# A two-layer decoder trunk on one core: sums of weights formed in place, a fourth landing buffer, one PSUM bank per step in the cross output projection, six pairs by seven products

## The chip, the core and the metric

The kernel runs on one core of a Trainium2 chip. A core has TensorE (matrix products, PE in the profile; PEld is its weight load), VectorE (DVE), ScalarE (ACT), GpSimd (POOL) and SyncE (SP, whose queue issues all DMAs here). The metric is the device time of one execution in microseconds, and less is better. Beside the times there is one profiled execution, whose rows this document quotes.

## What is computed

Two layers over 256 tokens of width 2048, all in float32:

```python
for l in range(2):
    h = rms_norm(x, attn_norm[l])
    q, k, v, ... = split(h @ w_in[l])                 # 6 MoBA, 4 differential, 6 DSA heads, an indexer
    x = x + concat(moba, diff, dsa) @ w_out[l]
    h, m = rms_norm(x, cross_norm[l]), rms_norm(mem, mem_norm[l])
    x = x + cross_attention(h @ cross_wq[l], m @ cross_wkv[l]) @ cross_wo[l]    # 4 heads, width 512
    u = rms_norm(x, ffn_norm[l]) @ ffn_w_up[l]        # 2048 -> 2 * 5504
    g, val = split(causal_conv3(u, ffn_conv_w[l]) + ffn_conv_b[l])
    x = x + (silu(g) * val) @ ffn_w_down[l]           # 5504 -> 2048
```

## The kernel before, in words

**Splitting.** Each operand of a large product is split into a rounded part and the rest: `hi` is made by ACT (line 79), `lo = raw - hi` by DVE (line 81). A product is then three matmuls: hi by hi, hi by lo, lo by hi. So every weight goes through one chain: SP issues the DMA into a `raw` buffer, ACT writes `hi`, DVE writes `lo`, PE reads both. There are three `raw`, three `hi` and three `lo` buffers of 8 KB per partition (`RAWS`, `HIS`), used in turn; a buffer is reused when its last reader is done. Activations are split in the same way (`parts`, lines 266 and 267, into tiles `a`).

**Order of the work.** The Tile framework keeps every engine's instructions in one fixed order, chosen when the program is built from priorities (the order of the code) and from when it expects data to be ready. Within an engine nothing overtakes: an instruction that waits holds back all behind it. Small chains (attention, norms) are written as generators; `step` runs one to its next `yield n`, and `tick` lets it go on after `n` groups of matmuls, so they lie between the matmuls of the next large product.

**Down projection** (`down`). `ffn_w_down` has 43 row blocks of 128: 21 pairs and one single. The output is made in two groups `g` of 1024 columns in each layer, so there are four groups in all. A group goes through the pairs in order, with the single one put in between. A *plain* pair takes 4 outputs x 2 row blocks x 3 = 24 matmuls of 512 columns. A pair whose number is in `SEVEN` goes by seven products of sums instead of eight (Winograd's form of Strassen's scheme): 7 x 3 = 21 matmuls, but DVE also forms four sums of weight blocks (lines 303 to 305, into a tile `sum` of its own, one buffer), sums of activations (298 to 301, tile `t`), and must split two sets of weights: the blocks themselves (`w`, 3 x 512) and the sums (`wt`, 4 x 512). Such a pair is called a seven below. A group ends with `combine` (lines 327 to 345: DVE adds the eight banks), and layer 0 then turns the result into the transposed residual `xT` (lines 1075 to 1080), while layer 1 writes it out by DMA (line 1064, on the SP queue like the loads).

**Output projections** (`residual`, `up_acc`). The transposed residual `xT` is updated in 8 steps of two column blocks. A step takes two PSUM banks out of four of the tag `mm`. In the cross output projection (`whole=True`) a step has 4 row blocks x 2 x 3 = 24 matmuls of 256 columns, and fills only half of each of its two banks; DVE adds each half bank to `xT` (line 437), then `take` splits the new `xT` for the next product (ACT line 180, DVE line 186) and sums its squares (ACT, then POOL line 408). After the 8 steps `factors` waits `G_R` ticks, multiplies the sums of squares by ones on PE (line 416) and forms the reciprocal root on DVE; after the cross output projection `spread` then brings it to all partitions (PE line 1007).

**Constants.** The convolution weights have one tile per layer (`cw0`, `cw1`), and the gains of the heads for both layers lie in three tiles (`gbd`, `gbs`, `gbm`) from the start on; `rope_table` multiplies them with sines and cosines on POOL. There are 8 tiles of the tag `t`, and 38 of the tag `k` (`slot`).

Of the kernel before, what the change touches and what calls it, by code (L numbers as in the profile page):

```python
# [10 lines left out]
F32 = mybir.dt.float32  # L11
# [9 lines left out]
L = 2  # L21
# [7 lines left out]
NEG = -1.0e30  # L29
GONE = -3.0e38  # L30
TOPK = 64
G_R, G_T, G_S, G_PT, G_DN = 3, 5, 1, 3, 3
FIRST_COL = 3328
KP, AP, RAWS, HIS = 38, 8, 3, 3
SEVEN = frozenset((2, 5, 8, 11, 14, 16, 18))
GW = 2 * CH


# [5 lines left out]
def hybrid_trunk(ctx: ExitStack, tc: tile.TileContext, x, mem, positions, attn_norm, w_in,  # L44
# [28 lines left out]
    def new_raw(a, n):  # L73
        return wp.tile([P, a, n], F32, tag="raw", name="raw", bufs=RAWS)

    def halves(src, a, n):

        hi = wp.tile([P, a, n], F32R, tag="hi", name="hi", bufs=HIS)
        nc.scalar.activation(hi, src, AF.Copy)  # L79
        lo = wp.tile([P, a, n], F32R, tag="lo", name="lo", bufs=HIS)  # L80
        nc.vector.tensor_tensor(lo, src, hi.bitcast(F32), OP.subtract)  # L81
        return hi, lo


# [41 lines left out]
    def attn_g(l):  # L126
        return gA[:, l * KT:(l + 1) * KT]

    def load_conv(l):
        cw = cst.tile([P, 4, 2 * NF], F32, name=f"cw{l}")  # L130
# [12 lines left out]
        return cw  # L143

# [83 lines left out]
    def up_acc(wview, runs, acts, order=None, whole=False):  # L228


        outs = [pmm() for _ in range(2)]
        order = order or EIGHTS
        first = True
        for gi, grp in enumerate(order):
            n = len(grp)
            hi, lo = load_split([wview[:, grp[0]:grp[0] + n, c:c + m] for c, m in runs], n, 2 * P)
            for j, k in enumerate(grp):
                last = gi == len(order) - 1 and j == n - 1
                for i in range(2):
                    wh, wl = hi[:, j, i * P:(i + 1) * P], lo[:, j, i * P:(i + 1) * P]  # L240
                    if whole:
                        nc.tensor.matmul(outs[i][:, :S], lhsT=wh, rhs=acts[k][:, :S], start=first, stop=False)
                        nc.tensor.matmul(outs[i][:, :S], lhsT=wh, rhs=acts[k][:, S:], start=False, stop=False)
                    else:
                        nc.tensor.matmul(outs[i], lhsT=wh, rhs=acts[k], start=first, stop=False)  # L245
                    ins = nc.tensor.matmul(outs[i][:, :S], lhsT=wl, rhs=acts[k][:, :S], start=False,  # L246
                                           stop=last)
# [22 lines left out]
    def down(act, wview, col, order):  # L270
# [16 lines left out]
        for i in order:  # L287
            m = width(i)
            k = 2 * i
            if i in SEVEN:  # L290
# [8 lines left out]
                                        OP.subtract)  # L299
                nc.vector.tensor_tensor(s4[:, 2, :], s4[:, 1, :], a4[:, 0, :], OP.add)  # L300
                nc.vector.tensor_tensor(s4[:, 3, :], a4[:, 2, :], s4[:, 2, :], OP.subtract)
                tt = wp.tile([P, 4, CH], F32, tag="sum", name="sum", bufs=1)
                nc.vector.tensor_tensor(tt[:, 0:2, :], b[:, 1::2, :], b[:, 0:1, :].to_broadcast([P, 2, CH]), OP.add)  # L303
                nc.vector.tensor_tensor(tt[:, 2, :], tt[:, 1, :], b[:, 1, :], OP.add)
# [7 lines left out]
                todo = {1: (A(0), B(0)), 2: (A(2), B(1)), 3: (Sx(3), B(2)), 4: (A(3), T(3)), 5: (Sx(1), T(0)),  # L312
                        6: (Sx(2), T(2)), 7: (Sx(0), T(1))}
                for q in (1, 2, 3, 5, 7, 6, 4):
                    ins = product(q, *todo[q])
            else:
# [92 lines left out]

    def factors(acc, rest=None):  # L410

        yield G_R
        pt = pat()
        for t in range(NT):
            for j in range(2):
                nc.tensor.matmul(pt[:, t:t + 1], lhsT=acc[:, j * S + t * P:j * S + (t + 1) * P],
                                 rhs=ones[:, 0:1], start=(j == 0), stop=(j == 1))
# [10 lines left out]
    def residual(acts, wview, order, g, tiles, rest=None, whole=False):  # L428

        acc = new_acc()  # L430
        for i in range(KT // 2):
            outs = up_acc(wview, [(2 * i * P, 2 * P)], acts, order[i], whole)
            pair = xT[:, 2 * i:2 * i + 2, :].rearrange("p k s -> p (k s)")
            if whole:
                for j in range(2):
                    v = xT[:, 2 * i + j, :]
                    nc.vector.tensor_tensor(v, outs[j][:, :S], v, OP.add)  # L437
# [70 lines left out]
        nc.gpsimd.tensor_copy(ropeI[:, 1, :, 0, 32:], s)  # L508

    TAB_W = {"d": 64, "s": 128, "m": 128}  # L510
    head_gain = {}
    for kind, g in (("d", diff_qk_gain), ("s", dsa_qk_gain), ("m", moba_qk_gain)):
        gb = cst.tile([P, L, 2, TAB_W[kind]], F32, name="gb" + kind)
        nc.sync.dma_start(gb.rearrange("p l a d -> p (l a d)"),
                          g.rearrange("l a d -> (l a d)").unsqueeze(0).to_broadcast([P, L * 2 * TAB_W[kind]]))
        head_gain[kind] = gb
# [15 lines left out]
    def rope_table(l, kind):  # L532

        w = TAB_W[kind]
        st, h = 128 // w, w // 2
        gb = head_gain[kind][:, l]
# [235 lines left out]
    for l in range(L):  # L772
# [239 lines left out]
        cw = load_conv(l)  # L1012


        up = ffn_w_up[l].rearrange("(k p) n -> p k n", p=P)
# [96 lines left out]
```

## Time and profile before

| | |
|---|---|
| median of 3 runs | 2567.83 us (2561.11 to 2570.95) |
| the profiled execution's own time | 2556.22 us |
| its span (first to last instruction) | 2554.4 us |
| PE busy | 98% |
| DVE busy | 75% |
| ACT busy | 53% |
| mean share of 16 DMA engines | 55.8% |
| mean granted TensorE clock | 0.997 |
| down projection, layer 0 and layer 1 | about 1039 to 1279 us, and 2307 to 2551 us |

The times are in us from the start of the span. In a list of groups a row has the line, the engine, the operation, the tiles (written<-read), the shapes and the count; behind the bar are the busy time, the mean in ns, and the idle time of the engine just before these instructions with what ended it. In a timeline a row has start, duration, engine, line and operation, and in square brackets how long the engine had been idle and what it waited for. In the chain of waits a row has the total, the count and the longest. A window row has the busy time of PE, its number of matmuls, the granted clock, the share of the DMA engines and GB/s. A matmul's duration is longer than its distance to the next, since matmuls are pipelined.

### The profile page before, as it was taken

The page shows a single profiled execution, that of the slowest core. Times are in us where ns is not written, and L with a number is a line of the kernel's source. Part 1 is how long each engine was busy: PE and PEld are TensorE (multiplying, and loading weights), DVE is VectorE, ACT ScalarE, POOL GpSimd, SP SyncE. Part 2 cuts the span into 40 slices and gives each one's busy share as a digit, 9 for nine tenths or more (in the row PEclk, how much of TensorE's full clock was granted, in tenths as well). Part 3 has the DMA queues.
Part 4 walks back from the last instruction along what each step waited for, and adds up shares of the span by engine and source line. Part 5 has one row for each costly group of instructions (what it writes and reads, how often), then busy time and mean ns, then how long its engine had stood idle before and what let it go on. Part 6 is the DMA issues. An engine that isn't in the chain of part 4 may idle for free. (4 is left out here: it accounts for less than half of the span.)

```text
span 2554.4 us, 34687 instructions
## 1 busy us (share of the span) xinstructions
PE 2514.4 (98%) x13402; PEld 2146.4 (84%) x13402; DVE 1910.2 (75%) x2982; ACT 1364.4 (53%) x1756; POOL 162.8 (6%) x177
## 2 busy tenths in 40 slices
PE   8999999999999999999999999999999999999999
PEld 7778888888888888877787788888888888888777
DVE  6876766677777777889968767666777777778888
ACT  5555565455554555556545555554555555555554
POOL 2210101010000000000041011010100000000000
PEclk9999999999999999999999999999999999999999
DMA  7545546555566656555654555564556665664554
GB/s 240 165 151 177 167 153 201 166 168 189 183 197 186 193 188 192 173 198 173 215 162 146 164 170 164 161 213 133 185 186 193 188 192 184 196 189 163 192 195 152
DMA packets 377705, 459.89 MB, mean 180 GB/s; under 512 B 10638, under 2 KB 331076, under 8 KB 377540
## 3 DMA queue, kind: packets, MB, share of 16 engines
q1 hardware_dynamic: 377540, 457.67, 55.8%
q8 instruction: 105, 1.72, 0.3%
q14 instruction: 60, 0.49, 0.1%
HBM read 455.54 MB, written 2.10 MB: 179 GB/s over the span
## 5 line engine op out<-in xcount | busy, mean ns | idle before, releaser
L81 DVE TENSOR_TENSOR lo<-raw,hi 128x2048 fp32r<-128x2048 f32 (+4 forms) x466 | 969.7, 2084 | 356.0 <-ACT hi L79 354.7
L245 PE MATMUL mm<-k,hi 128*128 128x512 f32 x3136 | 1098.4, 393 | 3.2 <-DVE xT L437 3.2
L79 ACT ACTIVATE hi<-raw 128x2048 fp32r<-128x2048 f32 (+4 forms) x466 | 811.2, 1744 | 434.5 <-PE mm L221 164.0
L246 PE MATMUL mm<-k,lo 128*128 128x256 f32 x3264 | 914.4, 280 | 0.1
L245 PEld LDWEIGHTS mm<-k,hi 128*128 128x128 f32 x3136 | 586.8, 187 | 133.2 <-issue 3.5
L246 PEld LDWEIGHTS mm<-k,lo 128*128 128x128 f32 x3264 | 617.1, 189 | 0.8 <-DVE lo L81 0.5
L220 PE MATMUL mm<-hi,k 128*128 128x512 f32 (+2 forms) x1088 | 413.8, 380 | 0.0
L221 PE MATMUL mm<-hi,k 128*128 128x512 f32 (+2 forms) x1088 | 404.3, 372 | 0.0
L222 PE MATMUL mm<-lo,k 128*128 128x512 f32 (+2 forms) x1088 | 401.6, 370 | 1.0 <-DVE lo L81 1.0
L220 PEld LDWEIGHTS mm<-hi,k 128*128 128x128 f32 x1088 | 206.3, 190 | 35.8 <-issue 3.3
L222 PEld LDWEIGHTS mm<-lo,k 128*128 128x128 f32 x1088 | 205.5, 189 | 36.1 <-DVE lo L81 1.8
L221 PEld LDWEIGHTS mm<-hi,k 128*128 128x128 f32 x1088 | 206.3, 190 | 32.6 <-issue 2.6
L285 PE MATMUL mm<-lo,a 128*128 128x512 f32 x548 | 216.4, 395 | 15.7 <-DVE lo L81 15.7
L283 PE MATMUL mm<-hi,a 128*128 128x512 f32 x548 | 214.6, 392 | 0.2 <-DVE t L1027 0.2
L284 PE MATMUL mm<-hi,a 128*128 128x512 f32 x548 | 214.4, 391 | 0.0
L1040 ACT ACTIVATE t<-t 128x256 f32<-128x256 f32 x86 | 35.7, 418 | 229.3 <-DVE t L1032 229.3
L285 PEld LDWEIGHTS mm<-lo,a 128*128 128x128 f32 x548 | 103.5, 189 | 43.2 <-DVE lo L81 21.9
L1027 DVE TENSOR_TENSOR t<-mm,t 128x256 f32<-128x256 f32 x172 | 68.8, 421 | 90.3 <-ACT t L1024 90.3
L1024 ACT ACTIVATE t<-mm 128x256 f32<-128x256 f32 x172 | 60.2, 375 | 142.2 <-PE mm L246 142.2
L408 POOL TENSOR_TENSOR k<-k,t 128x512 f32<-128x512 f32 x35 | 52.2, 1492 | 1138.0 <-ACT t L407 976.1
L283 PEld LDWEIGHTS mm<-hi,a 128*128 128x128 f32 x548 | 103.7, 189 | 21.6 <-issue 0.6
L284 PEld LDWEIGHTS mm<-hi,a 128*128 128x128 f32 x548 | 103.6, 189 | 21.8
(242 smaller groups left out, 2571.7 us busy)
## 6 DMA issues: line engine op xcount, KB each, us to landing
raw<-in_ffn_w_up_dram SPq DMA_DIRECT2D x168, 1024.0 KB, 5.1
raw<-in_w_in_dram SPq DMA_DIRECT2D x152, 512.0 KB, 4.5
raw<-in_ffn_w_down_dram SPq DMA_DIRECT2D x56, 1024.0 KB, 5.6
raw<-in_w_in_dram SPq DMA_DIRECT2D x20, 1024.0 KB, 5.0
raw<-in_w_out_dram SPq DMA_DIRECT2D x16, 1024.0 KB, 5.5
raw<-in_cross_wkv_dram SPq DMA_DIRECT2D x16, 1024.0 KB, 5.0
raw<-in_ffn_w_down_dram SPq DMA_DIRECT2D x32, 512.0 KB, 5.2
raw<-in_ffn_w_down_dram SPq DMA_DIRECT2D x56, 256.0 KB, 3.8
```

Of the source, the lines that this page charges most:

```text
L79: nc.scalar.activation(hi, src, AF.Copy)
L81: nc.vector.tensor_tensor(lo, src, hi.bitcast(F32), OP.subtract)
L220: nc.tensor.matmul(o, lhsT=xh, rhs=hi[:, j, :], start=first, stop=False)
L221: nc.tensor.matmul(o, lhsT=xl, rhs=hi[:, j, :], start=False, stop=False)
L222: ins = nc.tensor.matmul(o, lhsT=xh, rhs=lo[:, j, :], start=False, stop=last)
L245: nc.tensor.matmul(outs[i], lhsT=wh, rhs=acts[k], start=first, stop=False)
L246: ins = nc.tensor.matmul(outs[i][:, :S], lhsT=wl, rhs=acts[k][:, :S], start=False, stop=last)
L283: nc.tensor.matmul(bank[q], lhsT=x[0], rhs=w[0], start=first, stop=False)
L284: nc.tensor.matmul(bank[q], lhsT=x[1], rhs=w[0], start=False, stop=False)
L285: return nc.tensor.matmul(bank[q], lhsT=x[0], rhs=w[1], start=False, stop=left[q] == 0)
L1024: nc.scalar.activation(uv[:, S:], outs[i][:, S:], AF.Copy)
L1027: nc.vector.tensor_tensor(u, outs[i][:, :S], v, OP.add)
```

## The change

Seven edits, which belong together through the memory that they free and use:

1. The sums of weights are formed in place, in the `raw` buffer of the pair, after `w` is split; the tile `sum` goes. They are four additions of 512, and `wt` is split in two halves, each with one ACT and one DVE instruction.
2. `raw` and `hi` have four buffers, `lo` still three; `t` has seven instead of eight.
3. `SEVEN` is 2, 5, 8, 11, 14, 17 instead of 2, 5, 8, 11, 14, 16, 18: six pairs, three apart.
4. In the cross output projection a step uses one bank, its two halves beside each other, and DVE adds the whole bank to `xT` in one instruction.
5. `factors` waits five ticks instead of three, but three as before after the cross output projection.
6. There is one tile for the convolution weights, loaded anew in layer 1.
7. The heads' gains are loaded for each layer into `k` tiles; in layer 1 this puts three small DMAs between the loads of the indexer's second half.

```diff
-G_R, G_T, G_S, G_PT, G_DN = 3, 5, 1, 3, 3
+G_R, G_T, G_S, G_PT, G_DN = 5, 5, 1, 3, 3
-KP, AP, RAWS, HIS = 38, 8, 3, 3
-SEVEN = frozenset((2, 5, 8, 11, 14, 16, 18))
+KP, AP, RAWS, HIS, LOS = 38, 8, 4, 4, 3
+SEVEN = frozenset((2, 5, 8, 11, 14, 17))
...
-        return tp.tile([P, CH], F32, tag="t", name="t", bufs=8)
+        return tp.tile([P, CH], F32, tag="t", name="t", bufs=7)
...
-    def halves(src, a, n):
+    def halves(src, a, n, steps=(slice(None),)):
         hi = wp.tile([P, a, n], F32R, tag="hi", name="hi", bufs=HIS)
-        nc.scalar.activation(hi, src, AF.Copy)
-        lo = wp.tile([P, a, n], F32R, tag="lo", name="lo", bufs=HIS)
-        nc.vector.tensor_tensor(lo, src, hi.bitcast(F32), OP.subtract)
+        lo = wp.tile([P, a, n], F32R, tag="lo", name="lo", bufs=LOS)
+        for v in steps:
+            nc.scalar.activation(hi[:, v, :], src[:, v, :], AF.Copy)
+        for v in steps:
+            nc.vector.tensor_tensor(lo[:, v, :], src[:, v, :], hi[:, v, :].bitcast(F32), OP.subtract)
...
     def up_acc(wview, runs, acts, order=None, whole=False):
-        outs = [pmm() for _ in range(2)]
+        outs = [pmm() for _ in range(1 if whole else 2)]
+        own = [outs[0][:, i * S:(i + 1) * S] if whole else outs[i][:, :S] for i in range(2)]
...
     def down(act, wview, col, order):
-                tt = wp.tile([P, 4, CH], F32, tag="sum", name="sum", bufs=1)
-                nc.vector.tensor_tensor(tt[:, 0:2, :], b[:, 1::2, :], b[:, 0:1, :].to_broadcast([P, 2, CH]), OP.add)
-                nc.vector.tensor_tensor(tt[:, 2, :], tt[:, 1, :], b[:, 1, :], OP.add)
-                nc.vector.tensor_tensor(tt[:, 3, :], tt[:, 2, :], b[:, 2, :], OP.add)
                 a = parts(act[i], 4 * P)
                 w = halves(b[:, 1:4, :], 3, CH)
                 sx = parts(s, 4 * P)
-                wt = halves(tt, 4, CH)
+                for o, x, y in ((3, 0, 3), (0, 0, 1), (1, 3, 1), (2, 1, 2)):
+                    nc.vector.tensor_tensor(b[:, o, :], b[:, x, :], b[:, y, :], OP.add)
+                wt = halves(b, 4, CH, (slice(0, 4, 3), slice(1, 3)))
...
     def factors(acc, rest=None):
-        yield G_R
+        yield G_R if rest is None else G_R - 2
...
     def residual(acts, wview, order, g, tiles, rest=None, whole=False):
             if whole:
-                for j in range(2):
-                    v = xT[:, 2 * i + j, :]
-                    nc.vector.tensor_tensor(v, outs[j][:, :S], v, OP.add)
+                nc.vector.tensor_tensor(pair, outs[0], pair, OP.add)
...
+        if l:
+            head_gain.update(head_gains(l))
         for k in "dsm":
             tabs[k] = rope_table(l, k)
```

How this moves instructions shows at three places. The first is DVE's order in the down projection around a seven, in the middle of a group. Before, from the seven's split of its sums (`lo` of `sum_9877`) to the third addition for the next seven:

```order
L81 TENSOR_TENSOR lo_9895<-sum_9877,hi_9893 128x2048
L267 TENSOR_TENSOR a_9921<-k_7805,a_9920 128x512
L303 TENSOR_TENSOR sum_9994<-raw_9986 128x1024
L304 TENSOR_TENSOR sum_9994<-sum_9994,raw_9986 128x512
L81 TENSOR_TENSOR lo_9926<-raw_9918,hi_9924 128x2048
L267 TENSOR_TENSOR a_9955<-k_7994,a_9954 128x512
L81 TENSOR_TENSOR lo_9960<-raw_9952,hi_9958 128x2048
L305 TENSOR_TENSOR sum_9994<-sum_9994,raw_9986 128x512
```

And now, from the two plain pairs ahead of a seven to its end and the next pair:

```order
L83 TENSOR_TENSOR lo_10035<-raw_10028,hi_10034 128x2048
L271 TENSOR_TENSOR a_10065<-k_8544,a_10064 128x512
L83 TENSOR_TENSOR lo_10069<-raw_10062,hi_10068 128x2048
L271 TENSOR_TENSOR a_10105<-k_8733,a_10104 128x512
L83 TENSOR_TENSOR lo_10109<-raw_10096,hi_10108 128x1536
L271 TENSOR_TENSOR a_10113<-t_10100,a_10112 128x512
L310 TENSOR_TENSOR raw_10096<-raw_10096 128x512 x4
L83 TENSOR_TENSOR lo_10121<-raw_10096,hi_10120 128x2x512
L271 TENSOR_TENSOR a_10150<-k_8922,a_10149 128x512
L83 TENSOR_TENSOR lo_10121<-raw_10096,hi_10120 128x1024
L83 TENSOR_TENSOR lo_10154<-raw_10147,hi_10153 128x2048
```

The first additions of a seven (`sum_9994` from `raw_9986`) stood ahead of the splits of the two plain pairs that PE needs earlier (`lo_9926`, `lo_9960`); now nothing of a seven stands ahead of the plain pairs before it.

The second place is the SP queue at the change of groups in layer 1, where the output's four transfers (`out_0_dram`) stand among the loads of the second group. Before:

```order
L318 DMA raw_21327<-in_ffn_w_down_dram 128x2x1024
L1064 DMA out_0_dram<-k_20368 128x512
L1064 DMA out_0_dram<-k_20354 128x512
L292 DMA raw_21361<-in_ffn_w_down_dram 128x512
L1064 DMA out_0_dram<-k_20361 128x512
L1064 DMA out_0_dram<-k_20347 128x512
L293 DMA raw_21361<-in_ffn_w_down_dram 128x512
L294 DMA raw_21361<-in_ffn_w_down_dram 128x1024
```

And now:

```order
L320 DMA raw_21289<-in_ffn_w_down_dram 128x2x1024
L296 DMA raw_21323<-in_ffn_w_down_dram 128x512
L297 DMA raw_21323<-in_ffn_w_down_dram 128x512
L298 DMA raw_21323<-in_ffn_w_down_dram 128x1024
L320 DMA raw_21378<-in_ffn_w_down_dram 128x2x1024
L1073 DMA out_0_dram<-k_20333 128x512
L1073 DMA out_0_dram<-k_20319 128x512
L320 DMA raw_21412<-in_ffn_w_down_dram 128x2x1024
```

The three loads of the group's first seven (`raw_21361`, now `raw_21323`) stood behind two to four output transfers, and now stand ahead of them, with one plain pair more.

The third place is DVE in the cross output projection. Before, one step:

```order
L437 TENSOR_TENSOR xT_73<-mm_5056,xT_73 128x256
L437 TENSOR_TENSOR xT_73<-mm_5057,xT_73 128x256
L81 TENSOR_TENSOR lo_5191<-raw_5187,hi_5189 128x1024
L186 SCALAR_TENSOR_TENSOR k_5090<-xT_73,gains1_419,k_5090 128x256
L186 SCALAR_TENSOR_TENSOR k_5091<-xT_73,gains1_419,k_5091 128x256
```

And the same step now:

```order
L437 TENSOR_TENSOR xT_73<-mm_5052,xT_73 128x512
L83 TENSOR_TENSOR lo_5179<-raw_5176,hi_5178 128x1024
L188 SCALAR_TENSOR_TENSOR k_5084<-xT_73,gains1_419,k_5084 128x256
L188 SCALAR_TENSOR_TENSOR k_5085<-xT_73,gains1_419,k_5085 128x256
```

The order of the step stays, with one instruction less: in both, the weights that DVE splits right after the sum of a step are those of three steps later.

More of the change, by code (lines that the diff above doesn't have):

```diff
@@ L127, in attn_g @@
         return gA[:, l * KT:(l + 1) * KT]
+    cw = cst.tile([P, 4, 2 * NF], F32, name="cw")
     def load_conv(l):
-        cw = cst.tile([P, 4, 2 * NF], F32, name=f"cw{l}")
         cv = slot()[:2 * NF, :].rearrange("f (j p) -> f j p", p=P)
@@ L142, in load_conv @@
         step(rest())
-        return cw
     flows = []
@@ L241, in up_acc @@
                     if whole:
-                        nc.tensor.matmul(outs[i][:, :S], lhsT=wh, rhs=acts[k][:, :S], start=first, stop=False)
-                        nc.tensor.matmul(outs[i][:, :S], lhsT=wh, rhs=acts[k][:, S:], start=False, stop=False)
+                        nc.tensor.matmul(own[i], lhsT=wh, rhs=acts[k][:, :S], start=first and i == 0, stop=False)
+                        nc.tensor.matmul(own[i], lhsT=wh, rhs=acts[k][:, S:], start=False, stop=False)
                     else:
                         nc.tensor.matmul(outs[i], lhsT=wh, rhs=acts[k], start=first, stop=False)
-                    ins = nc.tensor.matmul(outs[i][:, :S], lhsT=wl, rhs=acts[k][:, :S], start=False,
-                                           stop=last)
+                    ins = nc.tensor.matmul(own[i], lhsT=wl, rhs=acts[k][:, :S], start=False,
+                                           stop=last and (i == 1 or not whole))
                 first = False
@@ L510, in hybrid_trunk, with head_gains @@
     TAB_W = {"d": 64, "s": 128, "m": 128}
[L511 to L516, printed above, removed]
+    def head_gains(l):
+        res, row = {}, None
+        for kind, g in (("d", diff_qk_gain), ("s", dsa_qk_gain), ("m", moba_qk_gain)):
+            n = 2 * TAB_W[kind]
+            if row is None or kind == "m":
+                row, o = slot(), 0
+            nc.sync.dma_start(row[:, o:o + n], g[l].rearrange("a d -> (a d)").unsqueeze(0).to_broadcast([P, n]))
+            res[kind] = row[:, o:o + n].rearrange("p (a d) -> p a d", a=2)
+            o += n
+        return res
+    head_gain = head_gains(0)
     lam = slot()
@@ L535, in rope_table @@
         st, h = 128 // w, w // 2
-        gb = head_gain[kind][:, l]
+        gb = head_gain[kind]
         tb = [slot()[:, :NT * 2 * w].rearrange("p (t a d) -> p t a d", t=NT, a=2) for _ in range(2)]
@@ L1010, in hybrid_trunk @@
         residual(coT, cwo, [[range(2), range(2, 4)]] + [[range(4)]] * 7, gB[:, (2 * L + l) * KT:(2 * L + l + 1) * KT], h3, spread, whole=True)
-        cw = load_conv(l)
+        load_conv(l)
         up = ffn_w_up[l].rearrange("(k p) n -> p k n", p=P)
```

4 lines of the change are left out of this document (2 added, 2 removed).

## The prediction

> **What bounds the kernel now.** I read the page first, then who PE waits for, then windows of time, then timelines round the longest waits.
>
> ```profile
> span 2554.4 us, 34687 instructions
> PE 2514.4 (98%) x13402; PEld 2146.4 (84%) x13402; DVE 1910.2 (75%) x2982; ACT 1364.4 (53%) x1756; POOL 162.8 (6%) x177
> ```
>
> PE is busy nearly always, so a gain can only come from the 40 us in which it stands, from matmuls that it need not do, or from its clock. Who it waits for, in us, times and longest:
>
> ```profile
> PE mm L285 <- DVE lo L81: 15.7, 14, 3.5
> PE at L416 <- POOL k L408: 4.9, 3, 2.2
> PE mm L245 <- DVE xT L437: 3.2, 2, 1.6
> PE mm L242 <- DVE xT L437: 2.1, 4, 0.5
> PE at L285 <- DVE lo L81: 1.6, 1, 1.6
> PE mm L222 <- DVE lo L81: 1.0, 2, 0.7
> PE at L1007 <- DVE t L1006: 0.8, 2, 0.5
> ```
>
> The first and the fifth row are the down projection: 17.3 us in 15 waits for the rest of a weight. Windows of PE, the first two of them without a wait, the others as long as the clock's own steps:
>
> ```profile
> 2000.00:2050.00 50.00, 50.00 (x291) 1.00 0.62 190
> 1050.00:1100.00 50.00, 50.00 (x222) 1.00 0.53 187
> 458.36:461.77 3.41, 2.43 (x11) 1.00 0.69 244
> 1164.91:1168.33 3.42, 0.38 (x2) 1.00 0.00 0
> 1168.33:1171.74 3.41, 2.92 (x7) 0.50 0.52 100
> 1287.79:1291.21 3.42, 1.90 (x12) 1.00 0.53 145
> 1291.21:1294.62 3.41, 3.41 (x9) 0.50 0.39 100
> 1728.11:1731.53 3.42, 2.20 (x14) 1.00 0.58 195
> 1731.53:1734.94 3.41, 3.41 (x10) 0.50 0.34 117
> 2376.65:2380.06 3.41, 0.94 (x4) 1.00 0.00 0
> 2380.06:2383.47 3.41, 3.41 (x9) 0.50 0.93 281
> ```
>
> In the down projection (second row) a matmul of 512 columns takes 50 / 222 = 0.226 us of PE. After each of four windows in which PE was busy for 2.2 us or less, the granted clock is 0.50 for 3.41 us; after 2.43 us it is not. A half-clock window has 9 matmuls where 3.41 / 0.226 = 15 would go, a loss of 6 x 0.226 = 1.4 us; four make 5.6 us that no wait shows.
>
> Why is the weight late? DVE, then PE, at the longest wait of layer 1:
>
> ```profile
> 2375.11 1.23 DVE L303 TENSOR_TENSOR sum<-raw 128x1024 f32<-128x1024 f32 x1 [2.66 <-DMA raw<-in_ffn_w_down_dram]
> 2376.37 0.69 DVE L304 TENSOR_TENSOR sum<-sum,raw 128x512 f32<-128x512 f32 x1
> 2376.98 2.28 DVE L81 TENSOR_TENSOR lo<-raw,hi 128x2048 fp32r<-128x2048 f32 x1
> 2379.18 0.68 DVE L267 TENSOR_TENSOR a<-k,a 128x512 fp32r<-128x512 f32 x1
> 2379.78 2.29 DVE L81 TENSOR_TENSOR lo<-raw,hi 128x2048 fp32r<-128x2048 f32 x1
> ```
>
> ```profile
> 2376.46 0.39 PE L284 MATMUL mm<-hi,a 128*128 128x512 f32 x1
> 2379.32 0.50 PE L285 MATMUL mm<-lo,a 128*128 128x512 f32 x1 [2.48 <-DVE lo L81]
> 2379.66 0.40 PE L283 MATMUL mm<-hi,a 128*128 128x512 f32 x1
> ```
>
> DVE stood 2.66 us for the transfer of the *next seven's* weights, because the first addition of that seven (L303) stands in its order ahead of the split that PE wants now; then the additions, then the split, and PE stands 2.48 us. The groups of DVE say that this is the rule, and give more prices:
>
> ```profile
> L81 DVE TENSOR_TENSOR lo<-raw,hi 128x2048 fp32r<-128x2048 f32 x360 | 825.3, 2294 | 290.9 <-ACT hi L79 290.0
> L81 DVE TENSOR_TENSOR lo<-raw,hi 128x1536 fp32r<-128x1536 f32 x44 | 77.2, 1754 | 13.9 <-ACT hi L79 13.9
> L303 DVE TENSOR_TENSOR sum<-raw 128x1024 f32<-128x1024 f32 x28 | 34.2, 1223 | 30.8 <-DMA raw<-in_ffn_w_down_dram 25.3 <-issue 4.9 <-DVE t L298 0.6
> L298 DVE TENSOR_TENSOR t<-k 128x256 f32<-128x256 f32 x28 | 11.1, 419 | 0.0
> L301 DVE TENSOR_TENSOR t<-k,t 128x128 f32<-128x128 f32 x28 | 7.7, 286 | 0.0
> ```
>
> L303 alone holds DVE up for 30.8 us in 28 sevens, 25.3 of them for a transfer.
>
> **The change part by part.** *In-place sums, fourth buffers, spacing.* A wait costs more than its idle time: PE's matmul at 2376.46 is shown as 0.39 long, though the next would start 0.226 later (0.16 hidden), and the first matmul after the wait takes 0.34 instead of 0.226 (0.11). So 15 waits cost 17.3 + 15 x 0.27 = 21.4 us.
>
> What remains of it? In the middle of a group nothing of a seven now stands ahead of the plain pairs before it. A triple (two plain pairs, one seven) costs DVE 2 x 2.29 + 1.75 + 2 x 1.22 (the halves of `wt`, by L303's row of the same size) + 4 x 0.69 + 4 x 0.68 (L304 and L267 in the timeline) + 0.42 + 2 x 0.29 = 15.3 us in 16 instructions. Each starts about 0.08 before its predecessor's shown end (2379.18 + 0.68 is 2379.86, the next starts at 2379.78), which leaves 14.0. PE needs (21 + 48) x 0.226 = 15.6. Two apart, as pairs 14, 16 and 18 are now, the same count gives DVE 11.1 against PE's 45 x 0.226 = 10.2: there DVE falls 0.9 behind at each step, three apart it has 1.6 to spare. `lo` still has three buffers. Counted from the end of the last seven on PE, the halves of the next `wt` can be split when the first plain pair is done, at 5.4; both are ready at 8.7, and PE wants them from 12.9 on. The tightest is the plain pair after the seven: its buffer comes free at 10.8, it is ready at 13.1, PE wants it at 15.6. I take no wait there; the fourth `raw` and `hi` cover the transfer and ACT, and without that cover the 2.7 of L303's wait would come back behind the seven's own split.
>
> It does not hold at the first seven of a group. The worst is layer 0's second group:
>
> ```profile
> 1157.77 1.23 DVE L303 TENSOR_TENSOR sum<-raw 128x1024 f32<-128x1024 f32 x1 [1.93 <-DMA raw<-in_ffn_w_down_dram]
> 1158.91 1.28 DVE L1078 TENSOR_TENSOR xT<-at,xT 128x512 f32<-128x512 f32 x2
> 1165.41 3.35 DVE L81 TENSOR_TENSOR lo<-raw,hi 128x2048 fp32r<-128x2048 f32 x1
> ```
>
> The block of `xT` from 1158.9 to 1165.4 stands ahead of pair 1's split, and PE waits 3.5 us. Now that split comes first: from 1155.8 (where the 1.93 began) 2.2 of split, 6.5 of block, 2.7 of its tail and 1.75 for `w` end at 1169.0, in time for PE, which reaches the seven at 1164.9 + 24 x 0.226 = 1170.3. The additions and the first half then end near 1173.3, wanted after nine matmuls at 1172.3; the second half comes after the next plain pair's split, near 1177.9, wanted at 1174.7. That is 1.0 + 3.2, with 0.54 for two waits 4.7. In layer 1 the loads of the first seven no longer stand behind the output's transfers, and no `xT` block lies there; I leave 1.3 for the three other group starts together. So 21.4 becomes 6.0: **-15.4**. Ends: nothing left (-21.4); or no gain, since `lo` has no fourth buffer (0).
>
> *Clock.* Two half-clock windows followed waits of L285, two those of L416. One may stay behind the 3.2 us above: 5.6 becomes 1.4, **-4.2** (ends 0 and -5.6). The Trainium skill, "TensorE: Matmul & The Clock Gate", section "Why this matters for your kernels", says that idle gaps over about 3 us bring the half clock back. The trace disagrees for gaps: waits of 2.48, 2.2 and under 2 us did it as well, so the busy time in a window decides here; by the rule three of the four would not be there, and the term would be -1.4 or less.
>
> *Five ticks.* A tick is 12 matmuls, two more give 24 x 0.226 = 5.4 us, over the longest wait of 2.2. All 4.9 go, with 0.11 each for the restart: **-5.2** (ends 0 and -5.2). Later is then the reciprocal root; the first that needs it comes after eight ticks, 8.1 us behind, against a dozen small DVE instructions of under 0.3 (L301's row) each and one split.
>
> *One bank per step.*
>
> ```profile
> 543.75 0.74 DVE L437 TENSOR_TENSOR xT<-mm,xT 128x256 f32<-128x256 f32 x2
> 544.41 1.21 DVE L81 TENSOR_TENSOR lo<-raw,hi 128x1024 fp32r<-128x1024 f32 x1
> 545.54 1.92 DVE L186 SCALAR_TENSOR_TENSOR k<-xT,gains,k 128x256 fp32r<-128x256 f32 x2
> 547.38 0.74 DVE L437 TENSOR_TENSOR xT<-mm,xT 128x256 f32<-128x256 f32 x2
> ```
>
> DVE has no idle time here; its step lasts 3.63 us, and PE stands 0.5 in each. With four banks ahead PE may run on, but the split weights of the next projection and the tiles of the last steps still come out of the same DVE queue, and PE meets its end at L1007, where it waits already. So it gains what DVE gains: 0.06 per step (one addition of 0.69 - 0.08 for the 0.66 of two), 0.5 per layer, and some 0.3 where a third `hi` was awaited. **-1.6** for both layers; ends 0 and 5.3 + 6 x 0.27 = 6.9 saved. I stay near the DVE row, since it is the full queue.
>
> *Six sevens.* 3 matmuls more in four groups: 12 x 0.226 = **+2.7**.
>
> *The rest.* The fourth `raw` starts the fourth load at once (L222's 1.0): **-0.5**, ends 0 and -1.5. Seven `t` tiles, one `cw`, gains by layer: 0. They are covered by the up projection, where PE's window shows no wait (first window row), and by POOL, which is busy 6%. The three small DMAs stand on SP's queue between loads; should they be held, four landed buffers of 5 us of PE each cover it. If that cover failed it would show as waits of L220 to L222; I allow 2 us.
>
> Sum: -15.4 - 4.2 - 5.2 - 1.6 + 2.7 - 0.5 = -24.2. The profiled execution took 2556.2 (span 2554.4 and 1.8 round it), 11.6 below the median of the runs; the terms are as many us in either, so 2532 for it and 2567.8 - 24.2 = **2544** for the median.
>
> **The rivals.** 0.5% is 12.8 us, about what a measurement of this kernel can tell from no change.
>
> *The waits for `lo` stay* (speaks for it: `lo` has three buffers as before, and each set of weights passes DVE in one order; against it: L303's 25.3 us of DVE idle, which cannot recur ahead of a plain pair). Then the first term is 0 and of the clock only L416's two windows go: -2.8 - 5.2 - 1.6 - 0.5 + 2.7 = -7.4, 2560: no change that can be told.
>
> *Nearly all goes*, the cross projection's waits too: -21.4 - 5.6 - 5.2 - 5 - 1 + 2.7 = -35, 2532. For it: PE wants the first weights of the up projection two steps later than now. Against it: the wait at L1007.
>
> *DVE becomes the bound in the down projection*: slower. The row at 1165.41 shows a split of 3.35 instead of 2.29, so something can stretch DVE's instructions; more loads and ACT work in flight, from the fourth buffers, could do it in every triple. Slower by 12.8 than before it is when a triple takes 37 / 24 = 1.5 us more than PE's 15.6, so when DVE's 14.0 is stretched to 17.1, by 22%. At 25% it is 24 x 1.9 = 46, minus 24.2: 2589. Against it: the mean of 360 such splits is 2294 ns, hardly over the 2.28 of single ones, in stages of every load.
>
> **How the numbers follow.** Forecast 0.64 (2537 to 2552 by itself), nearly all 0.14, waits stay 0.15, DVE bound 0.07. Faster by over 0.5% are the first two, 0.78; within, the third, 0.15; slower 0.07. The range leaves out the slow rival and a little at each end: 2532 to 2560.
>
> **What would show it.** Right: L285's waits at 6 us or less, the largest at the first seven of layer 0's second group; no DVE wait for a transfer ahead of a plain pair's `lo`; no wait at L416's line but the cross projection's; one half-clock window or none besides the last. Wrong: waits for `lo` at many sevens, or a DVE that is busy throughout the down projection with PE behind it; new waits of the mixer's products for slots or loads; waits that move from the cross projection's banks to its `lo`.

## The result and the profile after

The changed kernel takes 2534.9 us, the median of four runs (2529.17 to 2546.89), against 2567.25 before: a ratio of 0.9882, 95% interval 0.9837 to 0.9928. The profiled execution took 2529.17, with a span of 2527.0 against 2554.4, so 27.4 us less. First the page and the waits of PE (us, times, longest):

```profile
span 2527.0 us, 34675 instructions
PE 2507.3 (99%) x13414; PEld 2145.2 (85%) x13414; DVE 1897.4 (75%) x2982; ACT 1373.6 (54%) x1772; POOL 168.5 (7%) x177
```

```profile
PE at L142 <- DMA k<-in_ffn_conv_w_dram: 3.5, 2, 1.9
PE at L376 <- DMA k<-in_x_dram: 3.5, 4, 1.8
PE at L289 <- DVE lo L83: 1.4, 2, 1.1
PE at L142 <- DMA k<-in_ffn_conv_b_dram: 1.2, 2, 0.8
PE at L618 <- DVE mx L620: 0.9, 2, 0.5
PE at L418 <- POOL k L410: 0.8, 2, 0.4
PE mm L224 <- DVE lo L83: 0.7, 1, 0.7
PE at L287 <- ACT hi L81: 0.5, 1, 0.5
```

L289 is the line that was L285, L418 was L416, and `lo` is made in L83. The down projection's 17.3 us of waits for `lo` have become 1.4, all at one seven; the waits for `xT` in the cross output projection and those at its end (L1007, now L1016) are gone; and new is L142, where PE transposes the taps of the convolution and waits for their transfer.

Windows of PE, before and then after (width, busy time and matmuls, granted clock, DMA share, GB/s). The first pair lies in layer 1's down projection, the second in layer 0's output projection; the last two rows of before are two steps of the clock in a row, and the last two windows after lie ahead of half-clock windows:

```profile
2350.00:2500.00 150.00, 141.72 (x620) 0.99 0.56 192
360.00:440.00 80.00, 79.93 (x468) 1.00 0.53 168
2444.91:2448.33 3.42, 1.82 (x9) 1.00 0.80 264
2448.33:2451.74 3.41, 2.80 (x12) 1.00 0.06 22
```

```profile
2350.00:2500.00 150.00, 150.00 (x672) 1.00 0.60 201
360.00:440.00 80.00, 80.00 (x477) 1.00 0.58 176
564.16:567.58 3.42, 1.29 (x8) 1.00 1.05 309
1816.85:1820.27 3.42, 1.63 (x12) 1.00 0.42 103
```

From the first matmul of a stage to the first of the next, both layers together, the two traces give this (us; the attention stages hold the waits of the factors, which come after the start of a stage):

| stage | before | after | difference |
|---|---|---|---|
| start, attention projections, attention | 698.3 | 695.5 | -2.9 |
| output projection | 194.5 | 191.5 | -2.9 |
| memory's keys, cross queries and values | 161.6 | 157.3 | -4.3 |
| cross output projection and up projection | 1017.9 | 1020.3 | +2.3 |
| down projection | 482.1 | 462.5 | -19.7 |

The fourth row is where something was given back. SP's queue in layer 0 (start, duration over all rows of the line), and PE at the end of the cross output projection:

```profile
538.58 18.82 SPq L200 DMA_DIRECT2D raw<-in_ffn_w_up_dram  x6
557.45 0.43 SPq L135 DMA_DIRECT2D k<-in_ffn_conv_w_dram  x1
557.94 4.06 SPq L136 DMA_DIRECT2D k<-in_ffn_conv_b_dram  x1
```

```profile
562.81 1.05 PE L418 MATMUL at<-ones,k 128*128 128x1 f32 x8 [0.39 <-POOL k L410]
565.52 0.44 PE L142 MATMUL at<-ident,k 86*128 86x86 f32 x3 [1.66 <-DMA k<-in_ffn_conv_w_dram]
566.73 0.29 PE L142 MATMUL at<-ident,k 86*128 86x86 f32 x1 [0.77 <-DMA k<-in_ffn_conv_b_dram]
```

The taps' two small transfers stand behind six loads of the up projection, and the sixth waits until 557.4 for its buffer. Before, they stood behind four loads and went out at nearly the same moment, 558.03, but PE came to the ones matmuls at 568.3 and not at 562.8. So PE gained 5.5 us on transfers that hardly moved. The wait also leaves a window in which PE was busy for 1.29 us, and after it the granted clock is 0.50 for 3.41 us; layer 1 has the same with two half-clock windows.

### The profile page after: what moved, and what is told of

It is laid out like the page before. It is cut to its first block, busy times and chain, and to the rows that moved or that the text cites. A ratio compares the mean times of both kernels' runs of the same rounds, so it can differ in the third digit from the quotient of the medians.

```text
span 2527.0 us, 34675 instructions
## 1 busy us (share of the span) xinstructions
PE 2507.3 (99%) x13414; PEld 2145.2 (85%) x13414; DVE 1897.4 (75%) x2982; ACT 1373.6 (54%) x1772; POOL 168.5 (7%) x177
## 4 chain that ended last, share of the span: by engine, by line
PE 95%; DVE 3%; DMA 1%; issue 0%; ACT 0%; SPq 0%; DVEq 0%; ACTq 0%
PE mm L249 30%; PE mm L250 16%; PE mm L222 9%; PE mm L224 9%; PE mm L223 9%; PE mm L289 5%; PE mm L287 5%; PE mm L288 5%; PE at L618 1%; DVE lo L83 1%; PE at L289 1%; PE at L287 1%; PE at L288 1%; PE at L593 1%; DMA k<-in_ffn_conv_b_dram 1%; DVE k L188 1%
## 5 line engine op out<-in xcount | busy, mean ns | idle before, releaser
L83 DVE TENSOR_TENSOR lo<-raw,hi 128x2048 fp32r<-128x2048 f32 (+4 forms) x514 | 1040.4, 2028 | 434.7 <-ACT t L1033 208.0
L81 ACT ACTIVATE hi<-raw 128x2048 fp32r<-128x2048 f32 (+4 forms) x514 | 859.5, 1683 | 368.7 <-PE mm L223 178.1
L222 PE MATMUL mm<-hi,k 128*128 128x512 f32 (+2 forms) x1088 | 414.1, 381 | 0.0
L224 PE MATMUL mm<-lo,k 128*128 128x512 f32 (+2 forms) x1088 | 402.2, 370 | 0.7 <-DVE lo L83 0.7
L222 PEld LDWEIGHTS mm<-hi,k 128*128 128x128 f32 x1088 | 205.6, 189 | 37.1 <-issue 5.3
L224 PEld LDWEIGHTS mm<-lo,k 128*128 128x128 f32 x1088 | 205.0, 189 | 34.9 <-DVE lo L83 1.2
L287 PE MATMUL mm<-hi,a 128*128 128x512 f32 x568 | 221.5, 390 | 0.0
L288 PE MATMUL mm<-hi,a 128*128 128x512 f32 x568 | 221.4, 390 | 0.0
L289 PE MATMUL mm<-lo,a 128*128 128x512 f32 x568 | 221.2, 390 | 0.0
L1038 ACT ACTIVATE t<-t,cw 128x256 f32<-128x256 f32 x172 | 94.2, 595 | 118.2 <-DVE t L1037 118.2
L288 PEld LDWEIGHTS mm<-hi,a 128*128 128x128 f32 x568 | 106.7, 188 | 22.1
L289 PEld LDWEIGHTS mm<-lo,a 128*128 128x128 f32 x568 | 106.7, 188 | 22.1
L287 PEld LDWEIGHTS mm<-hi,a 128*128 128x128 f32 x568 | 106.7, 188 | 21.8
L1039 DVE SCALAR_TENSOR_TENSOR t<-t,cw 128x255 f32<-128x255 f32 x172 | 82.6, 481 | 34.1 <-ACT t L1038 34.1
```

Of the source, the lines that this page charges most:

```text
L81: nc.scalar.activation(hi[:, v, :], src[:, v, :], AF.Copy)
L83: nc.vector.tensor_tensor(lo[:, v, :], src[:, v, :], hi[:, v, :].bitcast(F32), OP.subtract)
L222: nc.tensor.matmul(o, lhsT=xh, rhs=hi[:, j, :], start=first, stop=False)
L224: ins = nc.tensor.matmul(o, lhsT=xh, rhs=lo[:, j, :], start=False, stop=last)
L287: nc.tensor.matmul(bank[q], lhsT=x[0], rhs=w[0], start=first, stop=False)
L288: nc.tensor.matmul(bank[q], lhsT=x[1], rhs=w[0], start=False, stop=False)
```

## The experiments

All times are medians, each with its ratio to the kernel before on the same chip. "Waits for lo" are those of the down projection's matmuls.

**Spacing alone.**

```diff
-SEVEN = frozenset((2, 5, 8, 11, 14, 16, 18))      # in the kernel before
+SEVEN = frozenset((2, 5, 8, 11, 14, 17))
```

> The kernel before with only the pairs by seven products changed: six, three apart, instead of seven. Theory A (the sums' own order is the cause: the first addition of the next seven stands on DVE ahead of the split that PE wants and waits there for a transfer): most waits for lo in the down projection stay, 10 us or more of the 17.3; with 2.7 us more of matmuls the span is 2547 to 2553 against 2554.4. Theory B (the spacing is the cause: DVE's work per seven does not fit two steps): the waits fall under 4 us and the span to about 2554.4 - 17 + 2.7 - 2 = 2538.

2559.7 us, ratio 1.0010 (0.9985 to 1.0036): nothing gained. A wait of PE, and the first addition of a seven on DVE (count, busy and mean, idle before it and its cause):

```profile
PE mm L285 <- DVE lo L81: 10.0, 7, 2.4
```

```profile
L303 DVE TENSOR_TENSOR sum<-raw 128x1024 f32<-128x1024 f32 x24 | 29.4, 1224 | 28.3 <-DMA raw<-in_ffn_w_down_dram 26.4 <-issue 1.9
```

The waits are fewer and longer, 10.4 us with one of 0.4 in another row, and L303 waits 26.4 us for transfers as before (25.3). The waits of 10 us or more are the first theory's. The span was 2562.7, over what either theory gave; 9.2 of it has a cause of its own (see the pace, below).

**The sevens of before in the changed kernel.**

```diff
-SEVEN = frozenset((2, 5, 8, 11, 14, 17))          # in the changed kernel
+SEVEN = frozenset((2, 5, 8, 11, 14, 16, 18))
```

> The changed kernel with the seven sevens of before (2, 5, 8, 11, 14, 16, 18). Theory A: waits for lo return only where sevens stand two apart, under 1 us each in four groups, 5 us at most with those at 1170; with 2.7 us fewer matmuls the span is 2525 to 2529 against 2527.0. Theory B (spacing is the cause): 10 us or more of waits for lo return, span 2534 or more.

2535.7 us, ratio 0.9921 (0.9889 to 0.9953).

```profile
PE at L289 <- DVE lo L83: 0.5, 1, 0.5
```

No wait came back, at pairs 16 and 18 neither. The span was 2533.9 with one of the slower up projections; less 9.2 it is 2524.7, 2.3 under the changed kernel's, for 12 fewer matmuls. So wider spacing bought nothing here and cost a pair by seven products in each group.

**Which buffer.** The changed kernel with `RAWS, HIS` = 3, 3, then 4, 3, then 3, 4 in place of 4, 4:

```diff
-KP, AP, RAWS, HIS, LOS = 38, 8, 4, 4, 3
+KP, AP, RAWS, HIS, LOS = 38, 8, 3, 3, 3            # or 4, 3, 3 or 3, 4, 3
```

> The changed kernel with three buffers of raw and hi instead of four. Theory A (the order of the sums is what counted): waits for lo in the down projection stay under 5 us, 2.5 of them at the first seven of layer 0's second group as now, and POOL's last addition still ends 7 us after the output projection's last matmul. Theory B (the fourth buffers carry it): DVE waits for transfers again behind the seven's own split, more than 8 us of waits for lo return, span 2535 or more.

> The changed kernel with four buffers of raw and three of hi. Theory A (the transfer has to be early: raw counts): waits for lo in the down projection stay at 5 us or less of the 15.5 that three and three left, span 2527 to 2530. Theory B (ACT has to run ahead: hi counts): 10 us or more of them return, span 2545 or more.

> The changed kernel with three buffers of raw and four of hi. Theory A (raw counts): 10 us or more of waits for lo, span 2545 or more. Theory B (hi counts): 5 us or less, span 2527 to 2530. If both this one and the one with four and three are over 10 us, both fourth buffers are needed.

3 and 3: 2556.4 us, ratio 0.9969 (0.9949 to 0.9989). 4 and 3: 2531.0 us, 0.9900 (0.9863 to 0.9938). 3 and 4: 2570.2 us, 1.0049 (1.0027 to 1.0072). The waits of PE for lo, with ACT's waits for the down projection's transfers, in that order (with four and three ACT has no such wait; with three and three the waits of PE at the taps are added):

```profile
PE mm L289 <- DVE lo L83: 12.6, 13, 1.2
PE at L289 <- DVE lo L83: 2.9, 8, 1.1
ACT hi L81 <- DMA raw<-in_ffn_w_down_dram: 69.2, 24, 4.4
PE at L142 <- DMA k<-in_ffn_conv_w_dram: 2.9, 2, 1.8
PE at L142 <- DMA k<-in_ffn_conv_b_dram: 1.0, 2, 0.5
```

```profile
PE mm L289 <- DVE lo L83: 0.9, 1, 0.9
PE at L289 <- DVE lo L83: 0.5, 1, 0.5
```

```profile
PE at L289 <- DVE lo L83: 11.0, 17, 1.8
PE mm L289 <- DVE lo L83: 4.5, 9, 0.6
ACT hi L81 <- DMA raw<-in_ffn_w_down_dram: 103.1, 29, 5.7
```

With three `raw` buffers and the sums in place, 15.5 us of the 17.3 are there: DVE no longer waits for a transfer ahead of somebody else's split, but ACT waits for the seven's, so the seven's own splits are late, and with three and three 12.6 of the 15.5 us are waits for the plain pair's split that stands right behind them. At the same spacing, with three buffers and the sums in a tile of their own (spacing alone), it was 10.4 us. So the new order by itself took no wait away. With four `raw`, all but 1.4 us goes, and the fourth `hi` isn't needed for that; without it PE waits 3.6 us at L418, behind the cross output projections, and 0.8 with it. Four buffers with the sums in a tile of their own were not tried. Three and four have one slower up projection (9.2 us, below); less that, their span of 2568.0 is still 4.5 us above the 2554.3 of three and three, and why was not followed up.

**Three ticks again.**

```diff
-        yield G_R if rest is None else G_R - 2     # in the changed kernel
+        yield 3
```

> The changed kernel with three ticks for the sums of squares everywhere. Theory A (POOL's chain of additions ends later than three ticks after the last step): waits of 1.4 to 2.2 us at the ones matmuls return at three places, with two half-clock windows, 8 to 10 us, span about 2536. Theory B (the fourth landing buffer has moved POOL's chain earlier too): under 2 us return, span 2529 or less.

2544.8 us, ratio 0.9957 (0.9936 to 0.9977); the profiled execution has a span of 2532.7, 5.7 more than the changed kernel.

```profile
PE at L418 <- POOL k L410: 4.1, 3, 3.3
```

Neither theory: 3.3 us come back at one place, behind layer 0's down projection, with two half-clock windows, and nothing at the two output projections. At those, POOL's last addition now ends 7.0 us after the start of the stage's last matmul, where it was 10.9 before. So two of the three waits would have gone without the ticks. The traces with fewer buffers say what moved POOL: with three `raw` or three `hi` that addition ends 9.2 to 11.1 us after, so both fourth buffers are needed for it.

**Two banks per step again.**

```diff
-        outs = [pmm() for _ in range(1 if whole else 2)]
-        own = [outs[0][:, i * S:(i + 1) * S] if whole else outs[i][:, :S] for i in range(2)]
+        outs = [pmm() for _ in range(2)]
+        own = [outs[i][:, :S] for i in range(2)]
...
-                nc.vector.tensor_tensor(pair, outs[0], pair, OP.add)
+                for j in range(2):
+                    v = xT[:, 2 * i + j, :]
+                    nc.vector.tensor_tensor(v, outs[j][:, :S], v, OP.add)
```

> The changed kernel with two banks per step in the cross output projection again (two additions of 256 columns in place of one of 512). Theory A (the bank is the cause): the six waits of about 0.5 and 1.6 us per pair of layers return, 5 us or more, and the steps last 3.6 us instead of 2.9. Theory B (the split that DVE makes at each step, 1.92 us in the kernel before and 0.88 in the changed one, sets the step, by whether it meets POOL's addition; the bank moves that only by chance): under 2 us of waits return, and the steps stay at 2.9 us while the splits stay at 0.88.

2536.6 us, ratio 0.9896 (0.9856 to 0.9936); the span was 2526.3.

```profile
PE mm L249 <- DVE xT L439: 1.0, 2, 0.5
```

One us of the 5.3 came back, and the waits at L418 went. In layer 0 the splits of the first four steps stay at 0.87 us. The second theory holds: the bank is not what freed this projection.

**No additions on POOL in the kernel before.**

```diff
-            take(i, g, tiles, acc)
+            take(i, g, tiles, acc, not whole)     # no gpsimd addition of squares where whole
```

> The kernel before without POOL's additions of squares in the cross output projection, so that the row factors behind it are wrong and 1.4 us of POOL work per step are gone. Theory A (DVE's second split stands still while POOL adds): that pair of splits takes 0.88 us instead of 1.92, DVE's step falls from 3.63 to 2.6 us, under PE's 2.88, and PE's 5.3 us of waits for xT in that projection go. Theory B (the splits are long for another reason, ACT reading the same tile or the loads in flight): they stay at 1.9 and PE waits as before.

2547.9 us, ratio 0.9934 (0.9914 to 0.9954). DVE's steps, with the row of each group that the split L186 forms in the kernel before and here:

```profile
542.33 0.75 DVE L438 TENSOR_TENSOR xT<-mm,xT 128x256 f32<-128x256 f32 x2
543.00 1.21 DVE L81 TENSOR_TENSOR lo<-raw,hi 128x1024 fp32r<-128x1024 f32 x1
544.13 0.87 DVE L186 SCALAR_TENSOR_TENSOR k<-xT,gains,k 128x256 fp32r<-128x256 f32 x2
544.92 0.74 DVE L438 TENSOR_TENSOR xT<-mm,xT 128x256 f32<-128x256 f32 x2
```

```profile
L186 DVE SCALAR_TENSOR_TENSOR k<-xT,gains,k 128x256 fp32r<-128x256 f32 x80 | 56.3, 742 | 7.7 <-ACT k L180 7.5
```

```profile
L186 DVE SCALAR_TENSOR_TENSOR k<-xT,gains,k 128x256 fp32r<-128x256 f32 x80 | 42.2, 566 | 7.7 <-ACT k L180 7.5
```

The pair of splits takes 0.87 us instead of 1.92, a step 2.59 instead of 3.63, and PE's waits at L242, L245 and L1007 are gone. So the split stood still while POOL added. The Trainium skill, "GPSIMD Engine Reference", section "1. Specifications", says that POOL's way into SBUF is shared with DVE and contended by DVE's instructions with two SBUF inputs; this split is one, and the runs agree, with 1.92 us beside the addition and 0.87 without it.

In the changed kernel the splits of the first steps come just before POOL's additions, as its timeline shows (the addition of the second step began at 539.09):

```profile
536.69 0.69 DVE L437 TENSOR_TENSOR xT<-mm,xT 128x512 f32<-128x512 f32 x1
537.30 1.22 DVE L83 TENSOR_TENSOR lo<-raw,hi 128x1024 fp32r<-128x1024 f32 x1
538.43 0.88 DVE L188 SCALAR_TENSOR_TENSOR k<-xT,gains,k 128x256 fp32r<-128x256 f32 x2
539.57 0.69 DVE L437 TENSOR_TENSOR xT<-mm,xT 128x512 f32<-128x512 f32 x1 [0.27 <-PE mm L250]
```

Later in this projection three pairs of splits still take 1.9 to 2.0 us. Which edit moved the first ones was not found.

**Taps early.**

```diff
+        conv = load_conv(l)          # issues the two transfers; rest() comes back and isn't stepped
         residual(coT, cwo, ...)
-        load_conv(l)
+        step(conv())
```

> The changed kernel with the two small transfers of the convolution's taps issued ahead of the cross output projection and not behind it. Theory A (they stand on SP's queue behind six loads of the up projection, which wait for landing buffers, and PE's transposes wait for them): 4.7 us of waits at the transposes and three half-clock windows of 1.4 us go, span 2518 to 2520 against 2527.0. Theory B (DVE, which finishes the splits of that projection late, is next in line): PE waits about as long for lo or for the factors there, span 2524 to 2528.

2536.4 us, ratio 0.9925 (0.9896 to 0.9954), and a span of 2538.2, which is more than 2527.0. Yet the waits at the taps and the half-clock windows went, as the first theory said, and the granted clock was 1.00 to the last matmul. The second theory has a part in it, a wait for the factors:

```profile
PE at L1016 <- DVE t L1015: 3.1, 2, 1.5
```

So 3.1 us of waits for the factors on DVE took the place of the 4.7 at L142. The time went to another place, which windows of 200 us in the two up projections show. First the changed kernel, then this one:

```profile
700.00:900.00 200.00, 200.00 (x1157) 1.00 0.61 190
2000.00:2200.00 200.00, 200.00 (x1156) 1.00 0.62 190
```

```profile
700.00:900.00 200.00, 200.00 (x1134) 1.00 0.59 184
2000.00:2200.00 200.00, 200.00 (x1133) 1.00 0.60 187
```

With no wait and the clock at 1.00, PE starts a matmul every 173.3 ns in the one and every 176.7 ns in the other, all through the projection once the small matmuls at its start are past. Over its 2752 matmuls that is 9.2 us, 18.3 for both layers; 2538.2 - 18.3 = 2519.9, within the 2518 to 2520 of the first theory. Spacing alone had one such projection in layer 0, the sevens of before one in layer 1, the run with 3 and 4 buffers one in layer 0.

**The changed kernel again.**

> The changed kernel again. Theory A (each up projection settles at one of two paces by chance, 9.2 us apart): times near 2529, 2538 and 2547 with little between them, and the profile's own pace of the two projections says which of them it is. Theory B (times spread by waits): times spread evenly, both projections at 173.3 ns per matmul.

2537.2 us, ratio 0.9918 (0.9891 to 0.9945). Its eight runs: 2528.99, 2530.02, 2530.37, 2537.17, 2537.18, 2537.63, 2546.01, 2548.14. Three levels, as the first theory said; the profiled execution (2530.37), both projections at the quicker pace, has a span of 2528.3. No execution of the two upper levels was profiled with this kernel.

**Another order of matmuls in the up and output projections**, with early taps and seven sevens:

```diff
-        for i in range(2):               # 512, 256, 512, 256
-            ... matmul(outs[i], lhsT=wh, rhs=acts[k])
-            ... matmul(own[i], lhsT=wl, rhs=acts[k][:, :S])
+        for i in range(2):               # 512, 512, 256, 256
+            ... matmul(outs[i], lhsT=hi[i], rhs=acts[k])
+        for i in range(2):
+            ... matmul(own[i], lhsT=lo[i], rhs=acts[k][:, :S])
```

> The changed kernel with the taps' transfers early, the seven sevens of before, and the matmuls of the up and output projections in another order (both of 512 columns, then both of 256). Each up projection has so far run at one of two paces, 173.3 or 176.7 ns per matmul, 9.2 us apart. Theory A (the pace hangs on how 512 and 256 columns alternate): one pace in both layers, span 2517 with the quick one. Theory B (it does not): either pace again, span 2517, 2526 or 2535.

2524.9 us (2524.01 to 2525.59 in four runs), ratio 0.9851 (0.9830 to 0.9871).

```profile
700.00:900.00 200.00, 200.00 (x1151) 1.00 0.61 189
2000.00:2200.00 200.00, 200.00 (x1151) 1.00 0.61 190
```

One pace in both layers, 174.2 ns, and its four runs lie within 1.6 us. It costs 2.3 us per projection against the quick pace and saves 6.9 against the other. So the first theory had the one pace right and its size wrong: of the 6.8 us by which the span, 2523.8, exceeds its 2517, 4.6 are the pace. What PE still waits for at the end of the cross output projection:

```profile
PE at L1018 <- DVE t L1017: 3.1, 2, 1.6
PE at L420 <- POOL k L412: 0.9, 2, 0.5
```

**Squares on DVE, the first seven later.**

```diff
-            nc.gpsimd.tensor_tensor(acc, acc, sq, OP.add)
+            (add or nc.gpsimd).tensor_tensor(acc, acc, sq, OP.add)     # add = nc.vector where whole
...
             order.insert(1 if g else NF // 4, NF // 2)
+            if g:
+                order[3:5] = order[4], order[3]
```

> The kernel with early taps, seven sevens and the other order of matmuls in the up projection, and two things more: the cross output projection's squares are added on DVE and not on POOL, and the first seven of the groups behind a first one comes one pair later. Theory A (POOL's addition holds DVE's split up): the splits take 0.88 us throughout, the factors come earlier, PE's waits at the ones matmuls and at the spread of the factors fall from 4.0 us to under 2, and the waits at the first seven of layer 0's second group from 1.3 to under 0.5: span 2520 to 2522 against 2523.8. Theory B (DVE is the bound there with its own work): the additions of 0.6 us in its queue cost what the splits gain, span 2523 to 2526.

2523.6 us (2521.12 to 2523.86), ratio 0.9867 (0.9836 to 0.9899); span 2521.8.

```profile
PE at L291 <- DVE lo L83: 2.7, 2, 2.2
PE at L1018 <- DVE t L1017: 0.5, 2, 0.3
```

The first half of the theory held: the 4.0 us at the factors became 0.5, though DVE has 0.6 us more work per step. The second did not: with the seven one pair later the waits for lo grew to 2.7, still behind a plain pair's split that DVE makes ahead of the seven's second half; why they are longer than before was not followed up. The span, 2521.8, is 2.0 us under that of the kernel before it, but that one ran on another chip, and the two ratios, 0.9867 and 0.9851, don't tell them apart.

## Why the prediction was right or wrong

The forecast of 2544 with 2532 to 2560 held 2534.9. On the profiled execution it said -24.2, and -27.4 came. Between the medians it is -32.3; both profiled executions had the quicker of two paces in both layers (last section), while the runs mix them, and how the runs of before divide was not taken apart. So that the median lies in the range is partly luck: two of its four runs, 2529.17 and 2529.74, lie below 2532. The nearness of the two sums is partly luck too, since terms that were off balance each other: the down projection gave some 5.6 us more than its terms with one half-clock window (-15.4, +2.7 and -1.4), and the stage of the cross output and up projections 3.9 less than its -1.6.

- *In-place sums, fourth buffers, spacing* (-15.4, and the sevens' +2.7). The stage gave -19.7, which holds both, and two half-clock windows. That the steady part would lose its waits was right, and so was the place of what is left, the first seven of layer 0's second group. Too much was left there: 4.7 us expected and 2.5 found (waits with their restarts), and of 1.3 at the other group starts nothing. The step that failed is the cause, "because the first addition of that seven (L303) stands in its order ahead of the split that PE wants now". With the order mended and three `raw` buffers, 15.5 us stay, and a fourth `raw` takes them. In the new order, then, the cause is the late transfer, and the order only chooses the split that has to wait for it. For the order of before this isn't shown, since a fourth `raw` was not tried with it. The sentence that "without that cover the 2.7 of L303's wait would come back behind the seven's own split" was the true one, for `raw` alone; and the 1.6 us of slack that three apart gives DVE bought nothing in the changed kernel.
- *Clock* (-4.2). All four windows went (the forecast left one), but three new ones stand behind the taps, so -1.4. Their windows, with 1.29 and 1.63 us busy, fit the reading that the busy time in a window decides, but as a threshold near 2.2 us it doesn't hold. In the kernel before, the window from 2444.91 was busy for 1.82 us and the clock behind it stayed at 1.00 (the rows above); with spacing alone one with 1.57 us did the same, behind a wait of 2.36. What decides stays open; the traces show that half-clock windows come behind single waits of 1.4 to 2.5 us, and not behind all of these.
- *Five ticks* (-5.2, and half of the clock's term). The two stages that hold these waits gave -2.9 and -4.3. The sum was nearly right and its reason held at one of three places only; at the other two the fourth buffers brought POOL's additions earlier.
- *One bank per step* (-1.6). All 5.3 us of waits for `xT` and the 0.8 at L1007 went. The step that failed is "I stay near the DVE row, since it is the full queue": of that row's 1.92 us, 1.04 were standing still beside POOL. A row of the same two splits, 0.88, stands at the start of the same projection.
- *The rest* (0). Here the wait that takes the place of the removed one was missed. It was looked for at L1007, and it came at L142: 4.7 us, with 0.8 at L418, and three half-clock windows. No edit touches the taps, but PE came 5.5 us earlier in layer 0 to transfers that went out at nearly the same moment. Six loads stand ahead of them on SP's queue where it was four; with three `raw` it is five, and PE waits there as well, 3.9 us with three `hi` and 4.8 with four. So the wait doesn't need the fourth `raw`. That the loads and small transfers on SP were "covered" was worked out for the gains alone.
- *Start* (-0.5): L222's 1.0 us became 0.7 (L224), so -0.3. The output projection's -2.9 had no term: 477 matmuls in 80 us where there were 468. In the same order of matmuls, runs with four `hi` had 477 too, with three 469 and 474.

Of the rivals, *nearly all goes* (2532) is nearest in time, but by other means: the cross projection's waits went and most of them came back at the taps. *Waits stay* is what three `raw` buffers do. DVE did not become the bound.

## What to carry to other kernels

When an engine waits for a transfer ahead of somebody else's work, change the buffer count and the order apart before you name one as the cause: here the new order with three landing buffers left 15.5 of 17.3 us, and one landing buffer more took nearly all of them. A stage that ends earlier meets the next small transfer that stands behind the loads on the queue, so look who needs those next. And before a busy DVE is called full, compare the same instruction at another place of the trace.

## What the hardware showed beside

The up projection's alternating matmuls of 512 and 256 columns run at one of two paces, 346.7 or 353.3 ns a pair, at a granted clock of 1.00 and without a wait; once a projection has begun, it keeps its pace. In the changed kernel this would make three levels of time, 9.2 us apart, and eight runs lie near 2529, 2537 and 2547; of the first four runs one, 2540.07, lies between. Grouped as 512, 512, 256, 256 they ran at one pace in all that was seen. Of the twelve profiled executions with the old order eight had the quicker pace in both layers, three in one and one in neither. What chooses it is open: no wait, half-clock window or buffer count goes with it in all of them.
